# Operand sums of the output projection made between memory regions, by a copying and an adding transfer, in a two-layer mLSTM and retention trunk

## The chip, the cores and the metric

The kernel runs on one core of one Trainium2 chip. The metric is the device time of one execution in microseconds (us); lower is better. It is taken over several executions, and the median is compared. One further execution was taken with the hardware profiler; its rows are what the text below reads.

The engines are named as in the profile: PE multiplies matrices, PEld loads PE's weights, DVE works on vectors, ACT applies activations and casts, POOL does small vector work and issues the transfers that add, and SP issues all other transfers. "SPq" or "POOLq" in a row is the sequencer of that engine. SBUF is the on-chip memory that the engines work on; "memory" below, where it is said of a transfer, is the chip's main memory (HBM, "dram" in tile names).

## The reference

Two layers run one after the other on 1024 tokens of width 1024. Each layer normalises, projects the tokens to eight heads' inputs, runs four mLSTM heads and four retention heads over the tokens, multiplies each head's normalised output by its gates, and projects the 2048 gated columns back to 1024:

```python
def reference(x, c, positions, w_ada, b_ada, norm_g, w_in, conv_w, conv_b,
              b_igate, b_fgate, gn_m, gn_r, w_out, final_g):
    ...
    for l in range(DEPTH):
        ada = c_act @ w_ada[l] + b_ada[l]
        shift, scale, gate = jnp.split(ada, 3, axis=-1)
        h = rmsnorm(x, norm_g[l]) * (1.0 + scale[:, None, :]) + shift[:, None, :]
        p = h @ w_in[l]
        ...
        y_m = jax.nn.sigmoid(mo) * head_layernorm(cell, gn_m[l], N_HEADS_MLSTM) * jax.nn.silu(mz)
        ...
        y_r = head_layernorm(ret, gn_r[l], N_HEADS_RET) * jax.nn.silu(rz)

        y = jnp.concatenate([y_m, y_r], axis=-1) @ w_out[l]
        x = x + gate[:, None, :] * y
    return rmsnorm(x, final_g)
```

All tensors are float32.

## The kernel before

**Products.** Every float32 product is made of three PE passes over operands that are split into a high part (`hH`, `wH`: a rounding cast, by ACT as a rule) and a low part (`hL`, `wL`: the rest, a subtraction by DVE). Both large projections use a scheme with seven products of half size in place of eight. It needs sums of operand blocks, named T1 to T4. For the output projection they are, for each of eight row blocks k of 128 rows (KT = 8 below):

T1 = (k, left) + (k, right); T2 = T1 + (k+8, right); T4 = T2 + (k+8, left); T3 = (k, right) + (k+8, right).

There are such sums of the weight `w_out` and of the gated head outputs `ydr`. Each block has 128 x 512 elements, 256 KB. The sums lie in memory as `wdr` (of the weight) and `fdr` (of the outputs) until the output projection loads them, as `raw` and `yf` tiles.

**Stages of a layer.** First the "border" products (one pair of columns and the first values, from a plain product); then 34 pairs of columns of the input projection, `pair()`, 84 matmuls of 128x512 each, in whose course the eight heads' attention runs; then the output projection in seven phases, `output()`. In the trace the row factors `rs` of the norm between the two layers stand on POOL at 1032.29 and 1073.47 us. In the pairs each head stores its queries, keys, values and gates to memory and loads them again.

**How the sums are made.** `weight_sums` makes the weight's, one sum after each pair; `early_job` makes the outputs' T1 for the first eight blocks as the heads get done; `late_job` makes T2 to T4 of the first two blocks. The other six blocks' T2 to T4 come from `last_rows` and `last_rows_2`, on DVE, and are left as they are. In `weight_sums`, `early_job` and `late_job` a sum is made in a tile named `fx`: SP loads the first operand into it, POOL issues a transfer that adds the second operand to the tile (`accum_op`), and SP stores the tile. T1, T2 and T4 of a block of the weight are made in one tile: it is held over three pairs or so, and each adding transfer waits for the store ahead of it to have read the tile.

**Tiles.** A tile belongs to a class, and a class has a few slots. `fx` is of class `h`, which has nine slots, H0 to H8. The same nine hold `wH` and `wL`, the split weights that PE needs next, two slots for each block. Within a class, slots are given in the order in which the program was recorded, so a `wH` recorded behind an `fx` waits for the slot that the `fx` gives back.

**What sets the order.** The kernel records its operations first, and `Program.order` then plans them: `simulate` runs a list schedule with a cost for each operation (`cost`) eight times over and keeps the shortest plan. Each engine then issues its operations in exactly the planned order; an operation that waits holds up all behind it on its engine. Off PE the ready operation that is due first is taken. After a transfer's planned end the plan leaves a reserve ahead of what uses it: `LATE` (1.5 us), or `FAR` (5 us) for the tiles that `record` marks as `far`. A slot is taken to be free at the planned end of its last user (`slot_free`), with no reserve.

The page's operations nearly all have one line number, L2068, since one loop issues the planned list; they are told apart by tile names.

Of the kernel before, what the change touches and what calls it, by code (L numbers as in the profile page):

```python
# [17 lines left out]
ALU = mybir.AluOpType  # L18
# [10 lines left out]
KT = D // P  # L29
# [165 lines left out]
class Program:  # L195
# [20 lines left out]
    def record(self, eng, fn, a, k):  # L216
        op = Op()
        op.eng, op.fn, op.a, op.k = eng, fn, a, k
        op.deps, op.allocs, op.seq = set(), [], len(self.ops)
        op.nom, op.stream, op.bytes, op.table = self.nom, None, 0, 0  # L220
        out = a[0]
        outs = [x for x in (out, k.get("accum_out")) if isinstance(x, Ref)]
        ins = [x for x in a[1:] if isinstance(x, Ref)]
        ins += [v for n, v in k.items() if isinstance(v, Ref) and n != "accum_out"]
        if (fn == "matmul" and not k.get("start")) or k.get("accum_op") is not None:
            ins.append(out)
        for x in ins:
            op.deps.update(o for o, area in x.buf.writes if touch(area, x.area))
        for x in outs:
            b = x.buf  # L230
            op.deps.update(o for o, area in b.reads if touch(area, x.area))
            if b.cleared is not None:
                op.deps.add(b.cleared)
            if b.cls is not None and b not in op.allocs:
                op.allocs.append(b)
        for x in ins:
            x.buf.reads.append((op, x.area))
            x.buf.users.add(op)
        for x in outs:
            x.buf.writes.append((op, x.area))  # L240
            x.buf.users.add(op)
            if fn == "memset":
                x.buf.cleared = op
        op.deps.discard(op)
        self.cost(op, out, ins)
        op.alts = []
        op.pin = self.pin and eng == "SP"
        op.far = isinstance(out, Ref) and out.buf.cls in ("q", "kk", "st", "dm")
        if eng == "PE":
            op.stream = self.stream  # L250
            if self.stream != "attn":
                self.nom += op.dur * self.scale
        self.ops.append(op)
        return op
# [8 lines left out]
    def cost(self, op, out, ins):  # L263
        eng, fn = op.eng, op.fn
        refs = [x for x in ins + [out] if isinstance(x, Ref)]
        n = max([elements(x) for x in refs] or [1])
        wide = sum(1 for x in ins if elements(x) == 1 and n > 2)
        psum = any(x.buf.cls in ("p", "a") for x in ins)
        op.lat = 0.12
        if fn == "dma_start":  # L270
            o = next(x for x in refs if not x.buf.dram)
            total = 4
            for s in o.shape:
                total *= s
            run = 4 * min(x.shape[-1] for x in list(op.a[:2]) if len(x.shape))
            op.bytes, op.dur = total, (0.95 if eng == "POOL" else 0.48)
            op.serve = 2.62e-6 * total if self.pin else 1.18e-3 * total / run * (9 + 0.0375 * run) / 16
            if any(name == "to_broadcast" for x in refs for name, _, _ in x.ops):
                op.serve += 1.0
        elif eng == "PE":  # L280
            n = elements(out)
            op.lat = 0.20
            if fn == "transpose":
                op.dur = 0.109
            elif op.a[1].dt == F32R:
                op.dur = max(0.064, 0.004 + 0.000444 * n)
            else:
                op.dur = max(0.222, 0.004 + 0.00167 * n)
        elif eng == "DVE":
            if fn == "tensor_tensor_scan":  # L290
                op.dur = 0.07 + 0.0021 * n
            elif fn in ("tensor_scalar", "tensor_copy", "memset") and not psum:
                op.dur = 0.07 + 0.00052 * n
            elif fn == "transpose":
                op.dur = 0.10 + 0.00104 * n
            else:
                op.dur = 0.07 + 0.00104 * n
            op.dur += 0.06 * wide
        elif eng == "ACT":
            op.dur = (0.055 if psum else 0.095) + 0.00084 * n + 0.095 * wide  # L300
        else:
            op.dur = 0.70 if len(op.a) > 3 and op.a[3] == ALU.pow else 0.45 if fn == "affine_select" else 0.16 + 0.00225 * n
        if eng == "ACT" and fn == "activation":
            f = op.a[2]
            op.table = 1 if f in (AF.Tanh, AF.Exp) else 2 if f == AF.Sin else 3 if f == AF.Ln else 0
# [84 lines left out]
    def simulate(self, queues):  # L390
# [10 lines left out]
        slot_free = {s: 0.0 for s in self.slot_width}  # L401
        slot_last = {}
# [63 lines left out]
        while done < len(ops):  # L466
            best, pick = None, None
            for e in engines:
                if e == "PE":
                    cand = None  # L470
                    for i, s in enumerate(self.STREAMS):
                        if at[s] < len(streams[s]):
                            o = streams[s][at[s]]
                            if o.known:
                                t = max(free[e], o.ready)
# [10 lines left out]
                if ready[e]:  # L486
                    t = free[e]
                elif pending[e]:
                    t = max(free[e], pending[e][0][0])
                else:  # L490
                    continue
                if e == "SP":
                    t = max(t, server[0] - 4.5)
# [11 lines left out]
            t = best  # L505
            if e == "PE":
                op = streams[s][at[s]]
# [6 lines left out]
            else:  # L514
                while pending[e] and pending[e][0][0] <= t + 1e-9:
                    o = heapq.heappop(pending[e])[2]
                    if o.start is None:
                        heapq.heappush(ready[e], (0.001 * o.seq - 1e4 if o.pin else o.late - o.boost, o.seq, o))
                op = None
                while ready[e]:  # L520
                    x = heapq.heappop(ready[e])[2]
                    if x.start is None:
                        op = x
# [3 lines left out]
                if e == "ACT" and op.table not in (0, table[0]):  # L527
                    same = [x for x in ready[e] if x[2].start is None and x[2].table in (0, table[0])
                            and x[0] < op.late + self.HOLD]
                    if same:  # L530
                        heapq.heappush(ready[e], (op.late - op.boost, op.seq, op))
                        x = min(same)
                        ready[e].remove(x)
                        heapq.heapify(ready[e])
                        op = x[2]
# [27 lines left out]
            for b in op.users_of:  # L563
                left[b] -= 1
                if left[b] == 0 and b.slot is not None:
                    slot_last[b.slot] = max(b.users, key=lambda u: (u.end, u.seq))
                    slot_free[b.slot] = slot_last[b.slot].end
                    freed += members[b.slot]
            if freed:
                grant_all(list(dict.fromkeys(freed)))  # L570
# [47 lines left out]
def tile_hybrid_trunk(ctx, tc, x, xt, c, positions, w_ada, b_ada, norm_g, w_in, w_gate, conv_w, conv_b,  # L618
                      b_igate, b_fgate, gn_m, gn_r, w_out, final_g, consts, out):
    nc = tc.nc  # L620
    x = x[0]
    out = out[0]
# [10 lines left out]
    V, A, G, PE, Q = (Engine(prog, n) for n in ("DVE", "ACT", "POOL", "PE", "SP"))  # L633
# [19 lines left out]
    def new(cls, n, name, dt=F32, slots=None):  # L653
        uid[0] += 1
        slots = classes[cls] if slots is None else slots
        b = Buf(cls, (P, prog.slot_width[slots[0]]), dt, f"{name}_{uid[0]}", prog.nom)
        b.slots = slots
        b.shape = (P, min(prog.slot_width[s] for s in slots))
        assert n <= b.shape[1], (cls, n)
        prog.bufs.append(b)  # L660
        return Ref(b)[:, 0:n]
# [59 lines left out]
    fdr = {n: [dram("fdr", (P, HALF)) for _ in range(KT)] for n in ("T1", "T2", "T3", "T4")}  # L721
    wdr = {n: [dram("wdr", (P, HALF)) for _ in range(KT)] for n in ("T1", "T2", "T3", "T4")}
# [843 lines left out]
        Q.dma_start(ydr[k * P:(k + 1) * P, i * HALF:(i + 1) * HALF].part((k, i)), g)  # L1566
        return yr, g

    def add_on(t, k, half, name, row):
        G.dma_start(t, y_source(k, half), accum_op=ALU.add)  # L1570
        Q.dma_start(fdr[name][row], t)

    def early_job(l, ks):
        for k in ks:
            y_half(l, k, 0)
            yield
            y_half(l, k, 1)
            t = new("h", 512, "fx")
            Q.dma_start(t, y_source(k, 0))
            add_on(t, k, 1, "T1", k)  # L1580
            yield

    def late_job(l, ks):
        for k in ks:
            y_half(l, k + KT, 0)
            yield
            y_half(l, k + KT, 1)
            t, u = (new("h", 512, "fx") for _ in range(2))
            Q.dma_start(t, fdr["T1"][k])
            Q.dma_start(u, y_source(k, 1))  # L1590
            add_on(t, k + KT, 1, "T2", k)
            add_on(u, k + KT, 1, "T3", k)
            add_on(t, k + KT, 0, "T4", k)
            yield

    direct = {}
# [27 lines left out]
    def y_source(k, half):  # L1624
        return ydr[k * P:(k + 1) * P, half * HALF:(half + 1) * HALF].part((k, half))

    def w_source(l, k, half):
        return w_out[l, k * P:(k + 1) * P, half * HALF:(half + 1) * HALF]

    def weight_sums(l):  # L1630
        for k in range(KT):
            for chain_ in (((None, 0, 0), ("T1", 0, 1), ("T2", 1, 1), ("T4", 1, 0)), ((None, 1, 1), ("T3", 0, 1))):
                t = new("h", 512, "fx")
                for name, kh, half in chain_:
                    src = w_source(l, k + KT * kh, half)
                    if name:
                        G.dma_start(t, src, accum_op=ALU.add)
                        Q.dma_start(wdr[name][k], t)
                        yield
                    else:  # L1640
                        Q.dma_start(t, src)

    PLAIN = {"11": (0, 0), "21": (1, 0), "12": (0, 1), "22": (1, 1)}
    PHASES = (("B11", "11"), ("T2", "T2"), ("T3", "T1"), ("T4", "22"), ("B21", "21"), ("T1", "T3"), ("B22", "T4"))
# [190 lines left out]
    for l in range(DEPTH):  # L1835
# [3 lines left out]
        if l:  # L1839
            ws, st, vw, banks = [[], []], {}, [], None  # L1840
# [3 lines left out]
        else:  # L1844
            ws, st, vw, banks = first
# [50 lines left out]
        n = 0  # L1896
# [209 lines left out]
```

## Time and profile before

| | |
|---|---|
| median of three executions | 2096.32 us (2096.01 to 2097.2) |
| the profiled execution, its own time | 2095.88 us |
| its span, first to last instruction | 2094.2 us |
| PE busy | 2051.9 us, 98% of the span |
| DVE busy | 1812.2 us, 87% |
| ACT busy | 1139.4 us, 54% |
| POOL busy | 206.1 us, 10% |
| bytes moved by transfers | 480.55 MB, 229 GB/s on average |
| granted PE clock | 0.994 |

How to read it: busy PE time is what the 9821 matmuls take, with ends that are modelled, so small gaps between them do not show. The rest of the span is idle PE. A row of a view that ends in "[0.89 <-DVE wL L2068]" says that the engine sat idle for 0.89 us ahead of this instruction, until DVE had made `wL`. "DMA wdr<-fx" as a releaser is the landing of that transfer.

### The profile page before, as it was taken

The numbers are of one execution on the slowest core, as the hardware profiler recorded it, in microseconds if no ns is written. First come the engines' busy times: TensorE is split into PE (matmuls) and PEld (weight loads), VectorE is DVE, ScalarE is ACT, GpSimd is POOL, SyncE is SP. The second block draws the span as 40 slices with busy tenths as digits, with TensorE's granted clock in tenths as the row PEclk, the third lists the DMA queues.
The fourth block names the chain that finished last, engine by engine and source line by source line (L and its number), as shares of the span: only waits on it lengthen the run. The fifth ranks groups of instructions, "written<-read, shape, count | busy, mean of one in ns | idle before, by whom it ended". The sixth has DMA issues, their size and how long they took to land.

```text
span 2094.2 us, 31188 instructions
## 1 busy us (share of the span) xinstructions
PE 2051.9 (98%) x9821; PEld 1705.8 (81%) x9821; DVE 1812.2 (87%) x3483; ACT 1139.4 (54%) x2124; POOL 206.1 (10%) x254
## 2 busy tenths in 40 slices
PE   6999999999999999999999999999999999999997
PEld 6888888778888888888888888888888888888886
DVE  7999999998887888894989989898978788888677
ACT  6755555456444444564666555566654434446544
POOL 0011110101001011011001000111010101110001
PEclk8999999999999999999999999999999999999999
DMA  9248676979796888999734699877768878989994
GB/s 302 80 138 222 186 214 177 254 229 265 228 269 191 246 257 233 272 318 339 231 117 117 174 238 256 232 219 202 228 195 241 232 227 226 271 250 301 333 319 149
DMA packets 508913, 480.55 MB, mean 229 GB/s; under 512 B 230706, under 2 KB 345146, under 8 KB 508748
## 3 DMA queue, kind: packets, MB, share of 16 engines
q1 hardware_dynamic: 493772, 451.29, 70.3%
q0 software_dynamic: 14976, 27.27, 7.9%
q8 instruction: 77, 1.26, 0.3%
q14 instruction: 88, 0.72, 0.1%
HBM read 322.16 MB, written 156.27 MB: 228 GB/s over the span
## 4 chain that ended last, share of the span: by engine, by line
PE 71%; DVE 13%; DMA 10%; issue 2%; SPq 2%; ACT 1%; POOL 0%; DVEq 0%; ACTq 0%; POOLq 0%
PE pp L2068 59%; PE pa L2068 12%; DVE wL L2068 3%; DVE acc L2068 2%; DVE x L2068 2%; DMA wdr<-fx 2%; SPq L2068 2%; DMA araw<-in_w_ada_dram 2%; DMA raw<-in_w_in_dram 1%; DVE raw L2068 1%; DVE rt L2068 1%; DMA fx<-in_w_out_dram 1%; DMA kk<-qdr 1%; DMA fdr<-fx 1%; DMA fx<-ydr 1%
## 5 line engine op out<-in xcount | busy, mean ns | idle before, releaser
L2068 PE MATMUL pp<-hH,wH 128*128 128x512 f32 x2416 | 958.2, 397 | 5.1 <-ACT hH L2068 2.8
L2068 PE MATMUL pp<-hL,wH 128*128 128x512 f32 x2416 | 957.0, 396 | 1.0 <-DVE hL L2068 1.0
L2068 PE MATMUL pp<-hH,wL 128*128 128x512 f32 x2416 | 955.4, 395 | 2.1 <-DVE wL L2068 1.9
L2068 PEld LDWEIGHTS pp<-hH,wL 128*128 128x128 f32 x2416 | 454.4, 188 | 106.9 <-DVE wL L2068 5.5
L2068 PEld LDWEIGHTS pp<-hH,wH 128*128 128x128 f32 x2416 | 454.4, 188 | 105.2 <-ACT wH L2068 2.9
L2068 PEld LDWEIGHTS pp<-hL,wH 128*128 128x128 f32 x2416 | 454.4, 188 | 101.6 <-DVE hL L2068 1.5
L2068 ACT CAST wH<-raw 128x512 fp32r<-128x512 f32 x515 | 315.5, 618 | 379.5 <-PE pp L2068 224.2
L2068 DVE TENSOR_TENSOR wL<-raw,wH 128x512 fp32r<-128x512 f32 x522 | 355.5, 685 | 106.6 <-ACT wH L2068 41.1
L2068 DVE SCALAR_TENSOR_TENSOR acc<-x,cols,acc 128x1024 f32<-128x1024 f32 x96 | 122.5, 1276 | 0.9 <-ACT acc L2068 0.7
L2068 POOL DMA_DIRECT2D fx<-in_w_out_dram x64 | 56.7, 886 | 592.7 <-DMA wdr<-fx 188.8
L2068 POOL TENSOR_TENSOR rsd<-va,mhalf 128x2 f32<-128x2 f32 x64 | 59.5, 930 | 562.1 <-DVE va L2068 494.4
L2068 PE MATMUL pa<-cf,q 128*128 128x258 f32 (+1 forms) x384 | 104.9, 380 | 1.9 <-DVE cf L2068 1.0
L2068 ACT ACTIVATE nd<-nd,nmu,rsd 128x256 f32<-128x256 f32 x117 | 65.3, 595 | 55.2 <-DVE nmu L2068 54.5
L2068 DVE TENSOR_TENSOR raw<-raw,raw 128x512 f32<-128x512 f32 x136 | 92.8, 684 | 0.6
L2068 PEld LDWEIGHTS pa<-q,kk 128*128 128x128 f32 x512 | 75.3, 191 | 8.7 <-issue 0.9
L2068 PEld LDWEIGHTS pa<-cf,q 128*128 128x128 f32 x384 | 69.1, 190 | 13.9 <-issue 1.8
L2068 PE MATMUL pa<-q,kk 128*128 128x128 f32 (+1 forms) x512 | 79.5, 301 | 0.5 <-DMA kk<-qdr 0.5
L2068 ACT CAST wH<-s 128x512 fp32r<-128x512 f32 x68 | 42.1, 619 | 67.7 <-PE pp L2068 35.0
L2068 DVE TENSOR_TENSOR hL<-yf,hH 128x512 fp32r<-128x512 f32 x90 | 60.7, 685 | 16.9 <-ACT hH L2068 15.3
L2068 ACT ACTIVATE yg<-yg,cols 128x512 f32<-128x512 f32 x63 | 45.5, 723 | 54.1 <-DVE yg L2068 53.5
L2068 PE MATMUL pa<-v,sd 128*128 128x258 f32 (+1 forms) x160 | 62.8, 393 | 2.1 <-ACT sd L2068 1.1
L2068 ACT CAST hH<-yf 128x512 fp32r<-128x512 f32 x89 | 53.6, 617 | 12.5 <-DMA yf<-fdr 4.9
(252 smaller groups left out, 2921.1 us busy)
## 6 DMA issues: line engine op xcount, KB each, us to landing
raw<-in_w_in_dram SPq DMA_DIRECT2D x280, 256.0 KB
araw<-in_w_ada_dram SPq DMA_DIRECT2D x96, 256.0 KB
fx<-in_w_out_dram POOLq DMA_DIRECT2D x64, 256.0 KB, 5.3
wdr<-fx SPq DMA_DIRECT2D x64, 256.0 KB
qdr<-acc SPq DMA_DIRECT2D x32, 512.0 KB
kk<-qdr SPq DMA_DIRECT2D x64, 256.0 KB
q<-qdr SPq DMA_DIRECT2D x64, 256.0 KB
ndr<-zt SPq DMA_DIRECT2D x128, 128.0 KB
```

Source lines behind the costliest of these rows:

```text
L2068: getattr(engines[op.eng], op.fn)(*[real(v) for v in op.a], **{n: real(v) for n, v in op.k.items()})
```

## The change

The tiles `fx` go. A new `sum_of(dst, one, two)` has SP copy the first operand from memory to the place of the sum in memory, and POOL issue a transfer that adds the second operand to that place. `weight_sums`, `early_job` and `late_job` use it; T2 starts from a copy of the stored T1, and T4 from a copy of the stored T2. In `record`, the `yg` tiles of class X (a head's output and its gate, loaded to be multiplied) get the long reserve `FAR`. In `simulate`, a slot of class `h` that a transfer uses last is taken to be free `LATE` after the transfer's planned end; once the `fx` tiles are gone, no transfer uses such a slot. In `cost`, a transfer without a tile is costed by its first operand, and a factor of 1 stands where an adding transfer could be costed apart.

```diff
@@ record
-        op.far = isinstance(out, Ref) and out.buf.cls in ("q", "kk", "st", "dm")
+        op.far = isinstance(out, Ref) and (out.buf.cls in ("q", "kk", "st", "dm") or out.buf.name[:2] == "yg" and out.buf.cls == "X")
@@ cost
-            o = next(x for x in refs if not x.buf.dram)
+            o = next((x for x in refs if not x.buf.dram), refs[0])
...
+            k_accum = op.k.get("accum_op") is not None
...
+            if k_accum:
+                op.serve *= 1
@@ simulate
-                    slot_free[b.slot] = slot_last[b.slot].end
+                    slot_free[b.slot] = max(u.end + (self.LATE if u.bytes and b.cls == "h" else 0.0) for u in b.users)
@@ the sums
-    def add_on(t, k, half, name, row):
-        G.dma_start(t, y_source(k, half), accum_op=ALU.add)
-        Q.dma_start(fdr[name][row], t)
-
     def early_job(l, ks):
...
-            t = new("h", 512, "fx")
-            Q.dma_start(t, y_source(k, 0))
-            add_on(t, k, 1, "T1", k)
+            sum_of(fdr["T1"][k], y_source(k, 0), y_source(k, 1))
             yield
 
     def late_job(l, ks):
...
-            t, u = (new("h", 512, "fx") for _ in range(2))
-            Q.dma_start(t, fdr["T1"][k])
-            Q.dma_start(u, y_source(k, 1))
-            add_on(t, k + KT, 1, "T2", k)
-            add_on(u, k + KT, 1, "T3", k)
-            add_on(t, k + KT, 0, "T4", k)
+            sum_of(fdr["T2"][k], fdr["T1"][k], y_source(k + KT, 1))
+            sum_of(fdr["T3"][k], y_source(k, 1), y_source(k + KT, 1))
+            sum_of(fdr["T4"][k], fdr["T2"][k], y_source(k + KT, 0))
             yield
...
+    def sum_of(dst, one, two):
+
+        Q.dma_start(dst, one)
+        G.dma_start(dst, two, accum_op=ALU.add)
+
     def weight_sums(l):
         for k in range(KT):
-            for chain_ in (((None, 0, 0), ("T1", 0, 1), ("T2", 1, 1), ("T4", 1, 0)), ((None, 1, 1), ("T3", 0, 1))):
-                t = new("h", 512, "fx")
-                for name, kh, half in chain_:
-                    src = w_source(l, k + KT * kh, half)
-                    if name:
-                        G.dma_start(t, src, accum_op=ALU.add)
-                        Q.dma_start(wdr[name][k], t)
-                        yield
-                    else:
-                        Q.dma_start(t, src)
+            d = {n: wdr[n][k] for n in wdr}
+            for name, one, two in (("T1", w_source(l, k, 0), w_source(l, k, 1)), ("T2", d["T1"], w_source(l, k + KT, 1)),
+                                   ("T4", d["T2"], w_source(l, k + KT, 0)), ("T3", w_source(l, k, 1), w_source(l, k + KT, 1))):
+                sum_of(d[name], one, two)
+                yield
```

Since the weight's sums no longer ask for a slot, the plan may put them wherever SP and POOL are free. Three places show where they stand now. In the rows `wdr_135` to `wdr_142` are T1 of the eight blocks, `wdr_143` to `wdr_150` T2, `wdr_151` to `wdr_158` T3, `wdr_159` to `wdr_166` T4; `raw<-in_w_in_dram` loads a block of a pair's weights.

The first place is SP at the start of layer 0's pairs. Before, one sum was begun among the loads of the pairs (`mdr` and `dm` belong to the first head's decay matrix):

```order
L2068 DMA raw_527_1168<-in_w_in_dram 128x512
L2068 DMA fx_494_1194<-in_w_out_dram 128x512
L2068 DMA raw_528_1208<-in_w_in_dram 128x512
L2068 DMA mdr0_10_1256<-mx_459_1245 4x512
L2068 DMA wdr_135_1271<-fx_494_1194 128x512
L2068 DMA raw_529_1277<-in_w_in_dram 128x512
L2068 DMA dm_544_1287<-mdr0_10_1256 128x256
```

Now, ahead of that place (`v0dr` and `gdr` are stores of the border's values and gates):

```order
L2062 DMA wdr_159_1091<-wdr_143_789 16x4096
L2062 DMA v0dr_100_1115<-bv_404_1049 128x512
L2062 DMA gdr_34_1177<-bz_395_1072 128x512
L2062 DMA gdr_35_1194<-bz_402_1004 128x512
L2062 DMA v0dr_101_1236<-bv_407_1133 128x512
L2062 DMA raw_526_1248<-in_w_in_dram 128x512
L2062 DMA wdr_160_1260<-wdr_144_797 16x4096
L2062 DMA wdr_161_1268<-wdr_145_811 16x4096
L2062 DMA wdr_162_1278<-wdr_146_821 16x4096
L2062 DMA raw_527_1286<-in_w_in_dram 128x512
```

All 32 copies of layer 0 stand on SP between the last loads of the border and the first head's `dm` loads, with the loads of the second and third pair among them; the row `wdr_160<-wdr_144` copies T2 to T4's place and waits for the adding transfer that makes T2. All 32 adding transfers of layer 0 stand on POOL ahead of its first work on `dm`.

The second place is SP in the middle of layer 0, about 457 to 463 us in the trace of before. There stood:

```order
L2068 DMA fx_1282_5068<-in_w_out_dram 128x512
L2068 DMA yg_1280_5121<-ndr_19_2909 128x512
L2068 DMA yg_1280_5121<-gdr_37_1746 128x512
L2068 DMA qdr_72_5015<-acc_1261_5043 128x1024
L2068 DMA araw_1415_5135<-in_w_ada_dram 128x512
L2068 DMA raw_1418_5142<-in_w_in_dram 128x512
L2068 DMA raw_1419_5149<-in_w_in_dram 128x512
L2068 DMA wdr_154_5154<-fx_1282_5068 128x512
L2068 DMA raw_1420_5172<-in_w_in_dram 128x512
```

Now at the same gate load `yg<-gdr_36` and the loads behind it (`ndr` and `st` belong to a head, `araw` to the next layer's conditioning):

```order
L2062 DMA fdr_111_4820<-fdr_103_4490 16x4096
L2062 DMA vdr_93_4651<-vt_1218_4813 32x4x256 x4
L2062 DMA yg_1238_4849<-ndr_18_2528 128x512
L2062 DMA yg_1238_4849<-gdr_36_1827 128x512
L2062 DMA araw_1271_4866<-in_w_ada_dram 128x512
L2062 DMA raw_1273_4881<-in_w_in_dram 128x512
L2062 DMA raw_1274_4890<-in_w_in_dram 128x512
L2062 DMA dm_1290_4897<-mdr0_10_1388 128x256
L2062 DMA raw_1275_4908<-in_w_in_dram 128x512
```

No `fx` row and no store or copy to `wdr` is left behind the first head's loads until the output phase of layer 0; of the sums only the outputs' (`fdr`) stay there.

The third place is POOL at the change of layers. `rs` is the row factor of the norm between the layers; `s` comes from DVE. Before, the two of them stood alone:

```order
L2068 TENSOR_TENSOR rs_2636_11291<-s_2635_11286,mhalf_3_70 128x4
L2068 TENSOR_TENSOR rs_2749_11714<-s_2748_11711,mhalf_3_70 128x4
L2068 MEMSET T4_2869_12208 128x512
L2068 DMA fx_2905_12296<-in_w_out_dram 128x512
L2068 MEMSET T4_2875_12364 128x512
```

Now layer 1's sums stand around them:

```order
L2062 DMA wdr_150_986<-in_w_out_dram 128x512
L2062 DMA wdr_151_658<-in_w_out_dram 128x512
L2062 DMA wdr_152_747<-in_w_out_dram 128x512
L2062 DMA wdr_153_1000<-in_w_out_dram 128x512
L2062 TENSOR_TENSOR rs_2721_11690<-s_2720_11685,mhalf_3_70 128x4
L2062 DMA wdr_154_1010<-in_w_out_dram 128x512
L2062 DMA wdr_155_1023<-in_w_out_dram 128x512
```

The second `rs` moved behind 19 adding transfers of layer 1, each of which waits for its copy and for the transfer eight ahead of it.

## The prediction

> **What bounds the kernel now.** I read the page's head first, then the windows by stage, then the timeline of PE for its stalls, and last the chain of waits behind each stall.
>
> ```profile
> span 2094.2 us, 31188 instructions
> PE 2051.9 (98%) x9821; PEld 1705.8 (81%) x9821; DVE 1812.2 (87%) x3483; ACT 1139.4 (54%) x2124; POOL 206.1 (10%) x254
> ```
>
> PE is busy for 98% of the span, so the change can only win what is left of 42.3 us, and lose without bound. The windows (us; busy us and instructions of PE, PEld, DVE, ACT, POOL; granted clock; DMA share; GB/s) say where the idle time lies.
>
> ```profile
> 0.00:50.00 50.00, 32.72 (x174) 29.52 (x175) 35.31 (x91) 30.93 (x74) 3.11 (x8) 0.86 0.95 312
> 50.00:150.00 100.00, 100.00 (x521) 84.58 (x520) 99.24 (x173) 67.60 (x108) 9.53 (x8) 1.00 0.34 99
> 150.00:500.00 350.00, 344.20 (x1637) 284.16 (x1636) 339.62 (x705) 194.10 (x363) 40.54 (x53) 1.00 0.78 222
> 500.00:900.00 400.00, 397.01 (x1941) 331.86 (x1940) 335.35 (x669) 192.64 (x376) 41.95 (x51) 1.00 0.85 242
> 900.00:1000.00 100.00, 100.00 (x440) 81.77 (x439) 68.84 (x114) 57.08 (x99) 12.82 (x14) 1.00 1.01 327
> 1000.00:1150.00 150.00, 150.00 (x751) 125.74 (x750) 140.40 (x255) 96.83 (x167) 11.99 (x9) 1.00 0.49 151
> 1150.00:1550.00 400.00, 398.10 (x1889) 330.04 (x1888) 357.63 (x680) 238.33 (x437) 42.20 (x63) 1.00 0.82 223
> 1550.00:1900.00 350.00, 348.09 (x1680) 290.07 (x1679) 288.74 (x553) 158.09 (x308) 34.68 (x39) 1.00 0.83 234
> 1900.00:2050.00 150.00, 150.00 (x666) 122.57 (x666) 115.87 (x197) 85.45 (x158) 3.25 (x3) 1.00 0.96 327
> 2050.00:2094.20 44.20, 31.81 (x138) 25.53 (x136) 31.16 (x57) 18.34 (x42) 6.04 (x8) 0.89 0.32 114
> ```
>
> Start (50 minus 32.72) and end (44.20 minus 31.81) hold 29.7 us of idle PE; the weights' sums are in neither, and the last 712 rows of PE are the same before and after. What the change can touch is the four middle rows with pairs and attention: 5.80 + 2.99 + 1.90 + 1.91 = 12.6 us. The DMA engines are 0.78 to 0.85 busy there, but only 0.34 busy in 50 to 150 us and 0.49 in 1000 to 1150 us. That is the room into which the sums move.
>
> The largest stalls of the middle, from the timeline of PE (start, duration, engine, line, operation; in brackets the idle time ahead and who ended it):
>
> ```profile
> 171.84 0.63 PE L2068 MATMUL pa<-ident,T 128*128 128x128 f32 x4 [0.77 <-DVE T L2068]
> 467.15 0.50 PE L2068 MATMUL pp<-hH,wL 128*128 128x512 f32 x1 [0.89 <-DVE wL L2068]
> 806.99 0.70 PE L2068 MATMUL pa<-cf,q 128*128 128x256 f32 x2 [0.90 <-ACT cf L2068]
> 865.86 0.39 PE L2068 MATMUL pa<-v,sd 128*128 128x256 f32 x1 [1.09 <-ACT sd L2068]
> 422.19 0.67 PE L2068 MATMUL pa<-cf,q 128*128 128x258 f32 x2 [0.66 <-DVE cf L2068]
> 537.84 0.50 PE L2068 MATMUL pp<-hH,wH 128*128 128x512 f32 x1 [0.75 <-ACT wH L2068]
> 1267.89 0.35 PE L2068 MATMUL pa<-v,sd 128*128 128x258 f32 x1 [1.00 <-DVE v L2068]
> 1817.19 0.38 PE L2068 MATMUL pa<-v,st 128*128 128x256 f32 x1 [1.45 <-DVE st L2068]
> 385.96 0.49 PE L2068 MATMUL pp<-hH,wH 128*128 128x512 f32 x1 [1.57 <-ACT wH L2068]
> ```
>
> Each is ended by DVE or ACT, which says little: the question is what held DVE or ACT. For the first four the chain of waits leads back to an `fx` tile:
>
> ```profile
> 161.74 4.23 DMA wdr<-fx
> 166.07 0.63 ACT wH L2068
> 461.69 4.62 DMA wdr<-fx
> 466.40 0.68 DVE wL L2068
> 855.27 4.79 DMA wdr<-fx
> 860.18 0.70 DVE wL L2068
> ```
>
> A split weight (`wH`, `wL`) waits for the slot that the store `wdr<-fx` has to give back first; the queue of DVE or ACT behind it is late for PE. The stall at 806.99 is the same with a store of the outputs' sum, and ACT's timeline shows the queue: `cf`, for which PE waits, stands behind a cast held for 2.69 us.
>
> ```profile
> 805.53 0.62 ACT L2068 CAST wH<-raw 128x512 fp32r<-128x512 f32 x1 [2.69 <-DMA fdr<-fx]
> 806.58 0.35 ACT L2068 COPY cf<-pa 128x256 f32<-128x256 f32 x1
> ```
>
> Over the whole kernel, the view of the tile `wH` (idle us of its engine, times) has
>
> ```profile
>   DMA wdr<-fx: 30.5, 19
>   DMA fdr<-fx: 19.4, 13
> ```
>
> 50 us in 32 waits, nearly all absorbed: only four reach PE, for 3.65 us.
>
> **The change part by part.** The price of a transfer first: the page's queue rows give packets, MB and share of the 16 DMA engines' span.
>
> ```profile
> q1 hardware_dynamic: 493772, 451.29, 70.3%
> q0 software_dynamic: 14976, 27.27, 7.9%
> ```
>
> SP's transfers: 70.3% of 2094.2 us over 451.29 MB, so 0.855 us of all engines for 256 KB. The adding transfers into a tile: 7.9% of 2094.2 over 27.27 MB, 1.59 us each. An add from memory to memory isn't in this trace. Its lower bound is 1.59 us, the nearest row; it reads the target as the old one did, only in another place. An upper bound comes from the 327 GB/s of the rows with DMA at 0.96 to 1.01: if that were the memory's limit, an add (two blocks read, one written) takes 3 x 0.262 MB / 327 GB/s = 2.40 us and a copy 1.60 us. I take 1.59 and 0.855, since in those rows the engines are full, so they don't show the memory as the limit; both ends go into the range.
>
> *Removed.* Each layer's 32 weight sums cost 48 SP transfers and 32 adds in the middle, 48 x 0.855 + 32 x 1.59 = 92 us of DMA time. Without them the share over 150 to 900 us falls from (350 x 0.78 + 400 x 0.85) / 750 = 0.82 to about 0.70. The `fx` tiles no longer take slots of class `h`: the four stalls go, 0.77 + 0.89 + 0.90 + 1.09 = **3.65 us**. Next late behind them: nothing of the sums, since the weight is next bounded by `raw`, loaded well ahead, so I take all of it.
>
> *Added.* 32 copies and 32 adds ahead of the first head, 32 x 0.855 + 32 x 1.59 = 78 us of DMA time, against 100 x 0.66 = 66 us free in 50 to 150 us; the rest runs into the stage behind. Layer 1's 78 us have 150 x 0.51 = 77 us free in 1000 to 1150 us. PE has no idle time in either row, and I cost them at nothing. What hides them is the weights loaded ahead; if that cover is gone, it is the slow rival's price below. In the order of SP, 40 copies wait for an add (T2 and T4 of the weights, and those of the outputs), and behind a waiting copy stand all loads of SP. On POOL the adds are queued ahead of the second `rs` at the layer change; rows of the timeline, the page's groups and its DMA issues:
>
> ```profile
> 1073.47 1.01 POOL L2068 TENSOR_TENSOR rs<-s,mhalf 128x4 f32<-128x4 f32 x1 [39.77 <-DVE s L2068]
> 1056.82 1.30 SPq L2068 DMA_DIRECT2D vraw<-in_w_in_dram  x2
> L2068 POOL DMA_DIRECT2D fx<-in_w_out_dram x64 | 56.7, 886 | 592.7 <-DMA wdr<-fx 188.8
> fx<-in_w_out_dram POOLq DMA_DIRECT2D x64, 256.0 KB, 5.3
> ```
>
> `rs` stands behind nineteen adds. The copies of the last five stand on SP behind the `vraw` loads, which before were out at 1058; with 5.3 us to land and 5 x 0.89 us for POOL to issue the adds, POOL is through at about 1068, 5 us ahead of 1073. I cost it at nothing; every us that copies or adds take more than these 5 delays the second half of the norm.
>
> *Outputs' sums.* Their 28 copies and adds stay in the middle. SP now waits for the add of T2 before it copies it to T4, which in two blocks of a layer makes four such waits. Cost 0; it can't gain beyond the stall at 806.99, counted above.
>
> *Less DMA traffic.* The stalls at 422, 538, 1268 and 1817 us lead back to other landings (values and states written and loaded again): 0.66 + 0.75 + 1.00 + 1.45 = 3.86 us. With the DMA share a seventh lower such a round trip gets shorter, but part of it is fixed. Bounds 0 and 3.86; I take a third, **1.3 us**.
>
> *The reserves.* The one on class `h` finds no transfer to act on once `fx` is gone. The one on `yg` asks for loads 3.5 us earlier. What it can win on DVE is
>
> ```profile
> DVE yg L2068 <- DMA yg<-gdr: 9.1, 14, 2.4
> ```
>
> 9.1 us in 14 waits of DVE, none the last step of a stall above. So 0 on PE; bounds 0 and a part of the 1.57 us at 385.96, where DVE's queue is late.
>
> *The new order.* Choices between ACT and DVE and the places of loads shift everywhere; the remaining stalls are reshuffled. The 12.6 us are what an old plan left over; a new one may leave other stalls: bounds 0 and +5 (about the sum of the five last stalls above, 5.43). I take **+0.5**.
>
> Sum: -3.65 - 1.3 + 0.5 = -4.45 us. The profiled execution's own time was 2095.88 us (span 2094.2 and 1.7 around it), 0.44 below the median of 2096.32, so 2095.88 - 4.45 = 2091.4.
>
> **Rivals.** *Given back* (the gain is hidden anyway). For it: DVE is 339.62 of 350 us busy in 150 to 500 us, where the largest idle time of PE lies, and the stall at 385.96 has no transfer behind it. Taking a wait out of DVE's queue there lets its next work start earlier but not end the stage earlier. Then the two stalls up to 500 us (1.66) stay in another place, and with the new order's +2 the result is 2095.88 - 2.0 + 1.7 = 2095.6, no change. Against: DVE in the other three rows has 10 to 18% free.
>
> *Slower: SP is held by copies that wait for adds.* The last copy of layer 0 is T4 of the eighth block. By then 24 copies and 18 adds have to be through from about 52 us, where SP comes free, plus one landing and issue, some 8 us: 52 + 24 x 0.855 + 18 x 1.59 + 8 = 109 us. Behind it stand loads of two more weight blocks. PE's run of projection matmuls in the chain of waits is
>
> ```profile
> 90.91 63.95 PE pp L2068 x276
> ```
>
> 0.232 us each; the block loaded behind the last copy is used 194 matmuls into it, at 90.9 + 194 x 0.232 = 136 us. Less landing, split and the `dm` loads ahead of it (12 us) it must be issued by 124 us. The slack is 15 us, and it is gone once an add takes 1.59 + 15 / 18 = 2.4 us. With the upper bounds, 24 x 1.60 + 18 x 2.40 + 60 = 142 us, 18 us late: 2091.4 + 18 = 2109. For it: each copy waits for the one eight ahead, and the add's price in memory isn't known. Against: the engines, not the memory, are full at 327 GB/s.
>
> The Trainium skill speaks for this rival: "DMA: Bandwidth & Descriptors", section Specifications, gives a limit of some 358 GB/s of HBM for one core. By it, as an estimate, 32 sums of five blocks read or written (41.9 MB) take 117 us in place of 78; no run here shows it.
>
> *It doesn't do what it says.* The order shows all weight sums out of the middle, so this holds only for the outputs': their 28 sums still hold SP there, in four places by a copy that waits for an add. Where one of these holds the loads of a head for 4 to 5 us, as a store `wdr<-fx` takes to land, one stall of 1 to 2 us comes back: 2093. The Trainium skill, "Perfetto Trace Analysis", section DMA Instruction — HWDGE, warns that the completion of a transfer can be surprisingly long when it writes to HBM. By that rule each such wait would grow; the trace doesn't agree so far, since the stores at 161.74 and 461.69 landed within 4.23 and 4.62 us.
>
> **How the numbers follow.** Forecast 2091.4, chance 0.48, with its own range 2084 (nearly all 12.6 us gone) to 2093; given back 0.32, 2093 to 2099; the outputs' waits 0.06, 2093; slower 0.14, 2099 to 2110. About 0.2%, 4.2 us, is what a measurement can tell from no change: faster means below 2092.1, slower above 2100.5. A small part of the forecast's case lies above 2092.1, and a small part of the rivals' below: faster 0.48, same 0.40, slower 0.12. A range of 2085 to 2101 leaves out about 1 in 10 on the slow side and less on the fast.
>
> **What would show it.** Right: no `fx` among the releasers; PE idle in 150 to 500 us down by about 1.7 and in 500 to 900 us by 2; DMA share near 1 from 50 to 150 us and near 0.70 behind it; PE still without idle time from 90 to 165 us and around 1000 to 1150 us. Wrong: a stall of PE between 120 and 170 us that ends with a load of a weight; adds that take over 2.4 us of the engines; a queue of DVE or ACT late in new places for as many us as went.

## The result and the profile after

The change makes the kernel **slower**: 2107.49 us (median of four, 2102.52 to 2108.96) against 2096.68 of before (four, 2096.01 to 2097.2); the ratio on record is 1.0042, 95% interval 1.003 to 1.0055 (the two medians alone give 1.0052). The profiled execution has a span of 2107.2 us, 13.0 more than before. The windows by stage, as shown of before:

```profile
0.00:50.00 50.00, 29.55 (x155) 27.16 (x156) 34.30 (x88) 30.97 (x74) 2.58 (x8) 0.83 0.94 312
50.00:150.00 100.00, 94.41 (x495) 80.08 (x494) 86.51 (x155) 59.77 (x98) 41.33 (x38) 0.98 0.93 231
150.00:500.00 350.00, 342.83 (x1620) 283.40 (x1619) 340.61 (x693) 192.10 (x358) 33.23 (x36) 1.00 0.66 189
500.00:900.00 400.00, 400.00 (x1963) 336.51 (x1963) 343.24 (x686) 198.27 (x382) 31.90 (x38) 1.00 0.75 212
1000.00:1150.00 150.00, 142.81 (x705) 118.73 (x704) 127.74 (x241) 92.70 (x163) 29.71 (x36) 0.97 0.90 258
1150.00:1550.00 400.00, 399.56 (x1892) 332.07 (x1891) 361.82 (x666) 242.09 (x433) 33.42 (x46) 1.00 0.72 195
1550.00:1900.00 350.00, 349.20 (x1685) 292.21 (x1684) 294.51 (x566) 161.43 (x310) 23.23 (x29) 1.00 0.71 198
```

Idle PE against before: the start 20.45 for 17.28 us, 50 to 150 us 5.59 for 0, 150 to 500 us 7.17 for 5.80, 1000 to 1150 us 7.19 for 0. In the other three rows with pairs 2.99, 1.90 and 1.91 became 0, 0.44 and 0.80. So in these three rows 5.6 us were gained; 17 us were lost at the start, from 50 to 500 us and at the change of layers. In 150 to 500 us, where 1.7 us were to be gained, idle PE grew by 1.4; the stall at 185.38 below alone is 2.89. DMA is where it was expected: 0.93 and 0.90 busy where the sums now are, 0.66 to 0.75 in the pairs. The five stalls of PE that make the loss (the first and the fourth had smaller forms before: 1.23 us at 43.89, 0.77 at 171.84):

```profile
42.72 0.59 PE L2062 MATMUL pa<-vwL,hH 128*128 128x264 f32 x1 [3.83 <-DVE vwL L2062]
89.83 0.39 PE L2062 MATMUL pa<-vwH,hH 128*128 128x264 f32 x1 [2.16 <-DVE g L2062]
112.61 0.50 PE L2062 MATMUL pp<-hH,wH 128*128 128x512 f32 x1 [3.26 <-DVE cb L2062]
185.38 0.63 PE L2062 MATMUL pa<-ident,T 128*128 128x128 f32 x4 [2.89 <-DVE T L2062]
1091.77 2.08 PE L2062 MATMUL pa<-dg,rmask 128*128 128x512 f32 x2 [6.63 <-DVE dg L2062]
```

A long stall costs more than its idle time. The starts of the projection's matmuls lie 0.23 us apart ahead of the stall at 1091.77 and 0.43 apart behind it, up to 1097.06:

```profile
1084.51 0.40 PE L2062 MATMUL pp<-hH,wL 128*128 128x512 f32 x1
1084.74 0.40 PE L2062 MATMUL pp<-hH,wH 128*128 128x512 f32 x1
1095.35 0.63 PE L2062 MATMUL pp<-hH,wL 128*128 128x512 f32 x1
1095.78 0.63 PE L2062 MATMUL pp<-hH,wH 128*128 128x512 f32 x1
```

The granted clock of 1000 to 1150 us is 0.97, before 1.00. PE is busy for 2053.2 us in all, before for 2051.9; these 1.3 us and 11.7 us more of idle time make the 13.0.

The last stall is the plainest. `dg` is made from `rs`; the timelines of DVE (`s`) and POOL around it:

```profile
1082.64 0.12 DVE L2062 TENSOR_SCALAR s<-pa 128x4 f32<-128x4 f32 x1
```

```profile
1078.94 2.50 POOL L2062 DMA_DIRECT2D wdr<-in_w_out_dram  x3 [8.52 <-DMA wdr<-wdr]
1086.87 0.83 POOL L2062 DMA_DIRECT2D wdr<-in_w_out_dram  x1 [5.43 <-issue]
1089.10 0.82 POOL L2062 DMA_DIRECT2D wdr<-in_w_out_dram  x1 [1.39 <-issue]
1089.64 1.34 POOL L2062 TENSOR_TENSOR rs<-s,mhalf 128x4 f32<-128x4 f32 x1
```

`s` is there at 1082.8, but `rs` starts at 1089.64, when the nineteenth add has been issued. Two kinds of wait made that late. Adds 15 to 17, the first row, waited 8.52 us for a copy to land; SP had issued that copy only at 1068.78, behind the last load of `vraw`:

```profile
1067.76 0.38 SPq L2062 DMA_DIRECT2D vraw<-in_w_in_dram  x1
1068.78 1.45 SPq L2062 DMA_DIRECT2D wdr<-wdr  x2
```

Then POOL stood before the last two adds, 5.43 and 1.39 us, with nothing that the profile names as releaser ("issue"). The view of `wdr` has the sum of such gaps: `issue`, 67.4 us in 33.

In the first burst it is SP and the landings. SP's timeline has the first T2 copies, which wait for adds (six take 11.07 us), and behind them the stores of the border's values; later the last copies:

```profile
62.87 11.07 SPq L2062 DMA_DIRECT2D wdr<-wdr  x6
74.04 1.05 SPq L2062 DMA_DIRECT2D v0dr<-bv  x2
92.37 0.33 SPq L2062 DMA_DIRECT2D v0dr<-bv  x1
108.67 2.59 SPq L2062 DMA_DIRECT2D wdr<-wdr  x4
```

These are two effects. The first stores of `v0dr` stood on SP behind the copies: ACT had made their `bv` by 69.7 us, and they were issued from 74.04. The store at 92.37 was issued as soon as its `bv` was made, but took 11.34 us to land, as the chain of waits shows:

```profile
92.37 11.34 DMA v0dr<-bv
```

Only at 103.71 may DVE write `hH` into the slot of `bv`; ACT had such a wait some 20 us before:

```profile
81.69 1.14 ACT L2062 CAST hH<-hf 128x512 fp32r<-128x512 f32 x2 [8.26 <-DMA v0dr<-bv]
103.73 0.43 DVE L2062 CAST hH<-hf 128x512 fp32r<-128x512 f32 x1 [5.97 <-DMA v0dr<-bv]
```

From these the chain of waits goes through DVE's queue to `cb` at 112.61 and on to the gates and `T` at 185.38. The adds of layer 0 run from 54.37 to 137.3 us, 2.6 us apart, with the DMA engines full (1.02 between 54 and 137).

### The profile page after: what moved, and what is told of

Its sections match the earlier page's. It is cut to its first block, busy times and chain, and to the rows that moved or that the text cites. A ratio compares the mean times of both kernels' runs of the same rounds, so it can differ in the third digit from the quotient of the medians.

```text
span 2107.2 us, 30955 instructions
## 1 busy us (share of the span) xinstructions
PE 2053.2 (97%) x9821; PEld 1711.7 (81%) x9821; DVE 1816.6 (86%) x3484; ACT 1146.1 (54%) x2125; POOL 216.3 (10%) x254
## 4 chain that ended last, share of the span: by engine, by line
PE 82%; DVE 8%; DMA 6%; issue 2%; SPq 1%; ACT 1%; POOL 0%; DVEq 0%; POOLq 0%; ACTq 0%
PE pp L2062 68%; PE pa L2062 14%; DVE wL L2062 2%; DVE acc L2062 1%; DMA araw<-in_w_ada_dram 1%; SPq L2062 1%; DVE x L2062 1%; DVE raw L2062 1%; DMA v0dr<-bv 1%; DMA q<-qdr 1%; DMA raw<-in_w_in_dram 0%; DMA xdr<-z 0%; DMA dm<-mdr 0%; DMA ydr<-yg 0%; DMA wdr<-in_w_out_dram 0%
## 5 line engine op out<-in xcount | busy, mean ns | idle before, releaser
L2062 ACT COPY ca<-pp 128x512 f32<-128x512 f32 x68 | 39.7, 584 | 64.9 <-PE pp L2062 64.7
L2062 DVE TENSOR_TENSOR hL<-yf,hH 128x512 fp32r<-128x512 f32 x90 | 60.7, 684 | 14.2 <-ACT hH L2062 12.8
L2062 POOL DMA_DIRECT2D wdr<-in_w_out_dram x64 | 53.6, 862 | 156.4 <-issue 67.4
L2062 POOL TENSOR_SCALAR_AFFINE_SELECT dm<-dm 128x256 f32<-128x256 f32 (+1 forms) x64 | 54.2, 869 | 138.1 <-DMA dm<-mdr 109.3
L2062 ACT COPY cb<-pp 128x512 f32<-128x512 f32 x67 | 39.0, 582 | 50.3 <-PE pp L2062 50.1
```

The lines of the kernel that those rows point to most:

```text
L2062: getattr(engines[op.eng], op.fn)(*[real(v) for v in op.a], **{n: real(v) for n, v in op.k.items()})
```

## The experiments

The theory named **burst** in the first expectations: the 32 sums of a layer, issued together, fill the DMA engines and hold SP's and POOL's queues while the border and the norm need them. `small` leaves the weight's sums incomplete and serves for timing alone; the other edits change only plan, order or descriptor memory. Ratios are to the kernel before on the same chip, whose median lay between 2098.61 and 2100.51 us there, so times in us are not to be set against the 2096.68 above.

**small**: same order of every engine, an eighth of each of the weight's adds.

```diff
+            whole = G.dma_start(dst, two, accum_op=ALU.add)
+            whole.a = (dst[0:16, :], two[0:16, :])
```

> The order of every engine is that of the changed kernel; only the adding transfers of the weight's sums are cut to 16 of their 128 rows, so that each moves an eighth (the sums of the weight are left incomplete). Theory 'burst' (the 32 sums of a layer, issued together, keep the DMA engines full for some 85 us and hold POOL's queue, and with it the border's stores, the first head's decay tiles and the second norm factor): the PE stalls at 89.83 (2.16 us), 112.61 (3.26), 185.38 (2.1 more than before) and 1091.77 (6.63) go, 14 us in all, and the median falls from 2107.5 to 2093 (2090 to 2097). The stall at 42.72 us (3.83) stays, since no sum is issued by then. Rival 'order' (the new plan has put the work of ACT, DVE and PE in a worse order): the order is the same, so 2103 to 2109. Rival 'price of a copy' (the 32 copies, not the adds, fill the DMA engines): half of the 14 us stays, about 2100.

Ratio 0.9943 (0.9926 to 0.9959), 2086.66 us: the loss goes, and more than was expected (2090 to 2097 us). Stalls between 50 and 200 us and at the norm are gone, that near 43 us stays (4.95 us). In the view of `wdr` no gap is put down to "issue". So with this order and with all the copies the kernel is faster than before: neither the order as such nor the 32 copies of a layer make the loss.

**held**: the copy of each of the weight's sums is planned only when PE's plan has reached the pair behind which it was recorded.

```diff
-            op.wait, op.ready, op.known = len(op.deps) + len(op.allocs), 0.0, False
+            op.wait, op.ready, op.known = len(op.deps) + len(op.allocs) + op.held, 0.0, False
...
+                    while held and held[0].nom <= op.nom:
+                        held[0].ready = max(held[0].ready, t)
+                        release(held.pop(0))
...
-                sum_of(d[name], one, two)
+                sum_of(d[name], one, two, True)
```

> The sums stay without tiles, but the planner holds the copy of each of the weight's sums back until PE's plan has reached the pair behind which it is recorded, one sum a pair as before. Theory 'burst': the stalls at 89.83, 112.61 and 1091.77 us go and that at 185.38 is back to under 1 us, the DMA share from 50 to 150 us is under 0.5; the four stalls behind fx tiles are gone as well, so the time is below that of before: 2092 (2087 to 2096). Rival 'price' (a sum made in memory is dear wherever it is made: 2.4 us and more of the DMA engines, and SP waits for it): 2100 to 2108, with stalls spread over the pairs. Rival 'order': another order again, 2092 to 2106, with the lost time in the queues of DVE and ACT.

Ratio 0.9979 (0.9966 to 0.9993). The four stalls of the burst are gone, and in 50 to 150 us the DMA share is 0.31:

```profile
50.00:150.00 100.00, 100.00 (x530) 85.33 (x529) 97.18 (x172) 68.41 (x109) 15.10 (x7) 0.99 0.31 94
1000.00:1150.00 150.00, 150.00 (x749) 125.74 (x749) 140.61 (x258) 98.60 (x169) 7.08 (x7) 1.00 0.46 147
```

So sums made in memory are no loss by themselves: spread out, they leave the kernel 0.2% faster. Of the 5.6 us of idle time that went from 500 us on in the changed kernel, some 2.2 go here too (1.29, 0.42 and 2.92 us are left in the three rows, one profile each); that the rest came with the emptier DMA engines in the pairs fits, but was not tested apart.

**nofar** and **before_far**: the reserve on `yg` taken out of the changed kernel, and put alone into the kernel before.

```diff
-        op.far = isinstance(out, Ref) and (out.buf.cls in ("q", "kk", "st", "dm") or out.buf.name[:2] == "yg" and out.buf.cls == "X")
+        op.far = isinstance(out, Ref) and out.buf.cls in ("q", "kk", "st", "dm")
```

> The changed kernel without the long reserve on the yg tiles; the sums stay bunched. Theory 'burst': the same stalls near 90, 112, 185 and 1091 us, 2107 (2102 to 2112). Rival 'reserve' (the longer hold of class X and the loads brought forward cost the time): the time falls to 2094 to 2099.

> The kernel before with only the long reserve on the yg tiles. Theory 'burst': the reserve is worth nothing on PE but changes the plan, 2096.5 (2093 to 2100). Rival 'reserve': 2102 to 2108.

1.0077 (1.0058 to 1.0097) and 1.0006 (0.9994 to 1.0018). The reserve isn't the cause. Without it the changed kernel came out somewhat worse than expected (2102 to 2112 us; 2114.95), with the same kinds of stall (6.75 us near 106, 7.91 before the norm).

**held_l0** and **held_l1**: held back in one layer only (`l == 0`, `l == 1` in place of `True`).

> Held back as in 'held', but only layer 0's sums; layer 1's stay bunched around the change of layers. Theory 'burst', added by place: the stalls at 89.83, 112.61 and 185.38 us are gone and that before the second half of the norm (near 1090 us, 6.6 us) is there; ratio to before 0.9979 + 6.6/2097 = 1.001 (0.999 to 1.003). Rival 'one place decides' (all of the loss comes from layer 0's burst, and what is late at 1091 would be caught up behind it): 0.998.

> Held back only in layer 1; layer 0's sums stay bunched from 50 us. Theory 'burst', added by place: some 7.5 us of stalls between 80 and 190 us, none at the norm; ratio 0.9979 + 7.5/2097 = 1.0015 (0.999 to 1.0035). Rival 'one place decides': 0.998, the early stalls caught up behind.

0.9993 (0.9983 to 1.0002) and 1.0016 (1.0004 to 1.0029). Layer 0's burst (`held_l1`) costs what was expected, with its three stalls. Of layer 1's (`held_l0`) only part was there: the second `rs` stands behind 17 adds in place of 19 and came in time for all but 0.44 us; 2.27 us were lost at 1125.69 instead. Where a burst hurts depends on which instructions the plan happens to put behind it.

**scratch512**: the same order, half the memory for the descriptors of POOL's transfers.

```diff
-    nc = _bacc.Bacc("TRN2", target_bir_lowering=False, num_devices=1, dynamic_dma_scratch_size=1024)
+    nc = _bacc.Bacc("TRN2", target_bir_lowering=False, num_devices=1, dynamic_dma_scratch_size=512)
```

> The changed kernel, every engine in the same order, with half the memory for POOL's descriptors (512 in place of 1024). POOL stood 67.4 us, in 33 gaps, ahead of the adds to wdr with nothing that the profile names as a releaser. Theory 'descriptor memory' (POOL can't write the next add's descriptors until an earlier add has been read): these gaps grow, beyond 100 us, and the adds come further apart; ratio 1.005 to 1.012. Rival 'engines' (the gaps only mirror full DMA engines): 60 to 75 us as before, ratio 1.003 to 1.0055.

Ratio 1.0473 (1.044 to 1.0506), 2198.66 us: far more than expected (1.005 to 1.012). The view of `wdr` has

```profile
  issue: 236.6, 53
```

and PE stalls of 15.87 and 34.94 us before the two halves of the norm, with the DMA engines at only 0.66 in 50 to 150 us. So most of these gaps are POOL's wait for room for descriptors, not a picture of full engines, and what stands behind the adds on POOL pays for them. The timelines of POOL agree: with 1024 three adds go out at the start of layer 0's burst and the fourth waits 5.34 us; with 512 they go singly, 5.1 us apart, about as long as one takes to land (median 4.8 us).

**pooldur**, **cost2**, **duronly**: prices of an add in the plan that are nearer to the trace, 1.62 us of DMA time in place of 0.81 and 2.1 us of POOL in place of 0.95, both and each alone (`pooldur` shown; `cost2` has only the factor, `duronly` only the duration).

```diff
-                op.serve *= 1
+                op.serve, op.dur = op.serve * 2, 2.1
```

> The changed kernel with the planner's price of an adding transfer corrected to what the trace shows: POOL held for 2.1 us each (0.95 before), DMA time twice as long. The sums stay bunched and the DMA engines stay full, but the second norm factor rs now stands behind 10 adds of layer 1 in place of 19; layer 0's adds are where they were. Theory 'POOL's queue' (what is late at the norm is rs, held in order behind adds): the stall near 1091 us falls from 6.6 to under 1.5 us, those at 90 to 190 us stay; ratio 1.001 (0.999 to 1.003). Rival 'full DMA engines' (loads and stores of the norm are late, whoever issues them): a stall of 4 us or more stays at the norm, ratio 1.003 to 1.005.

> The changed kernel; of the two corrections in 'pooldur' only the DMA time of an adding transfer is doubled in the plan (0.81 to 1.62 us), POOL's 0.95 us stays. The second rs stands behind 10 adds. Theory 'DMA price' (the plan's clock for transfers runs up to 32 x 0.81 = 26 us ahead of the chip's in a burst, and whatever is queued in order behind a late load or add is late): ratio 0.9955 as in 'pooldur' (0.993 to 0.998), no stall over 1.5 us between 80 and 190 us or near 1090. Rival 'POOL's time' (the 2.1 us of POOL did it): 1.000 to 1.005, with a stall at the norm or in 80 to 190 us.

> The other half: POOL held for 2.1 us each in the plan, the DMA time of an add as before (0.81). All 32 adds of layer 0 stand ahead of the dm tiles, and the second rs behind 20 adds. Theory 'DMA price': as the changed kernel, stalls in 80 to 190 us and one of over 3 us near 1090; ratio 1.002 to 1.006. Rival 'POOL's time': 0.9955 (0.993 to 0.998).

`pooldur` 0.9955 (0.9939 to 0.997), `cost2` 0.9958 (0.9944 to 0.9971), `duronly` 1.0027 (1.0013 to 1.0042). The expectation for `pooldur` (0.999 to 1.003) missed: the early stalls went too, though the adds are as bunched and the DMA engines as full. `cost2`, one number away from the changed kernel, shows why: **2091.95 us**, 0.42% below the kernel before, where the changed kernel was 0.42% above.

```profile
50.00:150.00 100.00, 99.01 (x527) 84.04 (x527) 95.82 (x174) 66.39 (x107) 31.81 (x36) 1.00 0.96 231
150.00:500.00 350.00, 346.78 (x1654) 286.91 (x1653) 342.43 (x711) 200.43 (x372) 27.70 (x40) 1.00 0.69 196
1000.00:1150.00 150.00, 150.00 (x749) 125.50 (x748) 140.19 (x257) 99.41 (x172) 29.82 (x36) 1.00 0.93 255
```

```profile
  issue: 43.8, 23
```

DMA is 0.96 and 0.93 busy, POOL still stands 43.8 us without a named releaser, and PE loses 1 us in the first burst and none in the second. In these two stretches the full engines cost next to nothing once the plan's price is right, since the order it lays out is another. The second `rs` stands behind 10 adds in place of 19 and waits only for `s`; and of the 14.2 us that ACT and DVE waited for landings of `v0dr`, the view of `v0dr` has 0.4 left:

```profile
1075.71 1.15 POOL L2062 TENSOR_TENSOR rs<-s,mhalf 128x4 f32<-128x4 f32 x1 [3.11 <-DVE s L2062]
  ACT hH L2062: 0.4, 1
```

In `duronly`, with the old DMA price, the early stalls are back (3.96 us near 89, 3.04 near 182). That at the norm is not, against the expectation: `rs` stands behind 20 adds, but starts at 1085.1, right after `s` (1084.9); why the adds were in time there wasn't followed. Each new price also gives a new plan with stalls of its own: `cost2`, `pooldur` and `duronly` have one in the output phase (2.75, 2.08 and 3.84 us near 935 to 942) that neither kernel has, and in `cost2` its chain of waits holds no add. So no single ratio is the worth of the price alone. What carries the reading is that both plans with the right DMA price come out 0.8 to 0.9% below the changed kernel, and the one without it 0.15%.

**before_pooldur** and **held_pooldur**: both corrected prices in the kernel before, and in `held`.

> The kernel before, with its fx tiles, and the same two corrected prices in its plan. It asks whether the gain of 'pooldur' comes with the sums in memory or with better prices alone. Theory 'both are needed' (without the fx tiles the sums can go where the DMA engines are idle; with true prices they do so without harm): the four kinds of stall behind fx remain, ratio 0.999 (0.997 to 1.002). Rival 'prices alone': 0.9955 to 0.997.

> True prices and the sums held back to one a pair. Theory: the early burst is no harm once the plan knows its price, and it frees the DMA engines in the pairs; held back they load them again (share 0.8 from 150 to 900 us in place of 0.7), so 0.9975 (0.995 to 1.000), above the 0.9955 of 'pooldur'. Rival 'the burst still costs': 0.993 or less, below 'pooldur'.

0.9983 (0.9972 to 0.9995) and 0.9965 (0.9953 to 0.9976). The better prices are worth something to the kernel before too, but less than with the sums in memory. Whether held or bunched is better under them isn't told apart: the intervals of `held_pooldur` and `pooldur` overlap.

## Why the prediction was wrong

It forecast 2091.4 us, faster; the time went the other way. By its steps:

- *The prices* were nearly right. The page after has

```profile
q1 hardware_dynamic: 481228, 436.61, 68.1%
q0 software_dynamic: 14976, 27.27, 8.0%
```

  that is 0.862 us for 256 KB on SP's queue (0.855 was used) and 1.62 for an add (1.59). Spread out among the pairs an add in memory was somewhat dearer, 1.79 us by the page of `held`; the 2.40 of the upper bound was never reached.

```profile
q0 software_dynamic: 14976, 27.27, 8.9%
```

- *Removed* and *less DMA traffic* held from 500 us on: none of the `fx` stalls is left, and the idle time fell by 5.6 us (2.99 + 1.90 + 1.91 less 0.44 and 0.80). In 150 to 500 us it rose by 1.4, since the stall at 185.38 outweighs the two that went.
- **The step that failed is *Added***: "PE has no idle time in either row, and I cost them at nothing." It set 78 us of transfers against 66 free and then counted only the weights' loads as cover. What had no cover was the border's own stores, whose slots are used again at once (`v0dr`, 14.2 us of ACT and DVE), and what stands on POOL behind the adds. The store that took 11.34 us to land stands against the 4.23 and 4.62 us on which the prediction set long landings aside. For POOL, 0.89 us of issue and one landing of 5.3 us were taken for the last five adds, with their copies out at 1058, so through at 1068 before the norm. They were through at 1089.9, 22 us late: some 11 us because `vraw` and with it the copies came out only at 1068.8, some 5 because the first copy took 10 us to land, and some 6.5 because POOL stood twice between the adds. `scratch512` shows what such a gap is, room for descriptors, a term that the sum put at nothing. The trace of before could hardly have told it: in the view of `fx`,

```profile
  issue: 19.2, 5
```

  but 13.48 of these 19.2 us are one gap, ahead of the add at 1492.40, and the add before it had been issued at 1478.02; none there takes over 9.1 us to land, so at most that one add was open and no room was missing. How the 8.3 us of the three early stalls divide between full engines and held queues was not measured apart.
- *The slower rival* had the size (2109) by luck, not the place or the mechanism. It looked for a stall between 120 and 170 us that ends with a load of a weight; none of the five lies there. It let SP's last copy be late beyond 124 us if an add took 2.4 us of the engines. The adds take 1.62 and SP was through at 111.3, against 109 by the first prices; what was 2.6 us apart were the issues of POOL. The cause below it is the plan: it prices an add at 0.81 us of DMA time, half of what it takes, so over 32 adds its clock for transfers is, as an estimate, some 26 us early (32 x 0.81), and each engine's fixed order is laid out on that clock. `cost2` against the changed kernel, with `duronly` beside it, shows that this price decides.
- *The start* (+3.2 us; 3.83 before 42.72) was not foreseen beyond the +0.5 for a new order. No sum has been issued by then, and it stays in `small`. It comes with the new order: the `vwL` that PE waits for releases it at 42.72 us, in the kernel before at 43.89, so it isn't later; but PE has stood at it since 38.9, before only since 42.7, with other products done first. Why the plan chose this was not tried, and whether it costs the kernel anything isn't shown: `small`, with 4.95 us there, is the fastest run.
- The limit of HBM was put into a sentence as the Trainium skill has it ("DMA: Bandwidth & Descriptors", section Specifications), with 117 us for a layer's sums as an estimate. The trace doesn't agree for this burst: the 32 sums of layer 0 were through within some 98 us of the first copy (50.45 us; the last add was issued at 136.49, and none took over 11.5 us to land), with other loads beside them, and the DMA engines were the full resource (1.02).

## What to carry to other kernels

A transfer moved into an idle stretch is free only if the plan that fixes the engines' order knows its price: where a fixed order is laid out on a clock, a burst put down at half its price makes much of what stands behind it late. Here one number in the plan decided whether the move lost 0.4% or won it. Before counting idle DMA time as cover, list what in that stretch waits for a landing, and what stands behind the issues on the issuing engine.

## What the runs showed of the hardware

- POOL can have only so many adding transfers open: with 1024 of descriptor memory it stood 67.4 us in 33 unnamed gaps ahead of 64 adds of 256 KB, with 512 it stood 236.6 us in 53 and the kernel took some 90 us more; with adds of an eighth none was recorded. The row "issue" on an engine that issues transfers can be such a wait, but need not be: the 13.48 us at 1492.40 in the kernel before are not.
- An add from memory to memory takes the DMA engines 1.62 us for 256 KB in the changed kernel and 1.79 in `held`, 1.9 to 2.1 times what 256 KB take on SP's queue (0.86 in both), and little more than one into a tile (1.59); these are averages of POOL's queue, in which 92 of 104 transfers are such adds. Its landing went from a median of 5.5 us where the adds were spread out (`held`) to 7.4 us in the burst.
- Behind a PE stall of 6.63 us the matmuls' starts lay 0.43 us apart in place of 0.23 for some 5 us.
